# An encoder block on one core: two by two blocks with seven products in the in-projection, x turned on the host, and attention beside other matmuls

## The chip, the core and the metric

The kernel runs on 1 core of one Trainium2 chip. Its time is the device time of one launch in microseconds (us); work on the host does not count. Before the change it took 2023.58 us, the median of 3 runs (2023.04 to 2024.13). Five engines work side by side, each in the order of its own program: TensorE (PE, matmuls and transposes), VectorE (DVE), ScalarE (ACT), GpSimd (POOL) and SyncE (SP, which here only starts DMA transfers). They wait for each other through semaphores.

## The reference, cut to what matters

One layer of a bidirectional encoder on 512 tokens of width 2048, all in float32. Two mixers read one projection of the normalised input: A has 8 query heads on 2 key heads with rotary angles on normalised q and k; B has 8 heads whose three dilated windows are merged by their softmax denominators. Heads have 128 columns.

```
h = rmsnorm(x, g_mix[layer])
proj = jnp.einsum('bsd,de->bse', h, w_in[layer])            # 512 x 2048 by 2048 x 4608
qa, ka, va, qb, kb, vb = jnp.split(proj, offs, axis=-1)     # 1024, 256, 256, 1024, 1024, 1024 columns
...
out_a = rmsnorm(mixer_a(qa, ka, va, g_q_a[layer], g_k_a[layer]), g_out_a[layer])
out_b = rmsnorm(mixer_b(qb, kb, vb), g_out_b[layer])
mixed = jnp.concatenate([out_a, out_b], axis=-1)
x = x + jnp.einsum('bse,ed->bsd', mixed, w_out[layer])      # 2048 x 2048
h2 = rmsnorm(x, g_ffn[layer])
gate, up = jnp.split(jnp.einsum('bsd,df->bsf', h2, w_gate_up[layer]), 2, axis=-1)   # 2048 x 11264
x = x + jnp.einsum('bsf,fd->bsd', jax.nn.silu(gate) * up, w_down[layer])            # 5632 x 2048
return rmsnorm(x, g_final)
```

## The kernel before

**Three products for one.** Every float32 operand is split in two: ACT copies it rounded to the type fp32r (the high part), and DVE subtracts that copy from the original (the low part). `mm3` (L194 to L198) then multiplies high by high, high by low and low by high into one PSUM bank. So each weight tile costs one ACT pass, one DVE pass and three matmuls for each 128 rows of tokens.

**Seven products for eight.** The gate/up and down stages go further. They take their matrices as 2 x 2 blocks and compute the four blocks of a product with seven block products instead of eight, named m1 to m7. The sums of blocks on the activation side are made once per pair of rows (`pair_sums`, L656), those on the weight side for every tile (`ColBlock.weights`, L778). A form's 12 matmuls (two rows, two halves of the tokens, `mm3`) make one unit, and three pairs of PSUM banks, z, y and x, collect the seven products in the order of `CHAIN`; ACT copies a bank out (`snap`) where another block needs it too, and DVE adds the rest.

**The in-projection** does not do this. `in_chunk` (L534) takes 512 columns of w_in at a time, nine chunks, each 16 units (one for each 128 rows of w_in) of 12 matmuls for the four tiles of tokens. During the first chunk `x_transposes` (L256) turns x with PE, 128 columns at a time, ACT and DVE scale it by g_mix and split it into `arena`, and ACT and POOL sum its squares; the norm's factor is applied when a chunk leaves PSUM (`post_kvA`, `post_qA`, `post_vB`, `post_qkB`). The order is: k and v of A, q of A (two chunks), v of B (first half), q and k of B for heads 0 to 3 (two chunks), v of B (second half), q and k of B for heads 4 to 7.

**Attention** runs in the gaps between units. `push_head` (L489) puts the tasks of a head on a list, `side`, and the main loop takes one task after each unit: m0 (turn q; last value product of the head before the last, `fin`), tk (turn k), and four steps `ms(i)`, each with the scores of 128 queries of this head (`score`), the turning of a quarter of the weights of the head before (`pt`) and that head's value product before (`pv`). In `score`, DVE takes the row maximum out of PSUM, ACT the exponential with the row sum, DVE its reciprocal and the scaling of the row:

```
nc.vector.tensor_tensor_reduce(p, ps, mask[:, lo:lo + S], -1.0, 3e38, op0=OP.add, op1=OP.min, accum_out=nmx)
nc.scalar.activation(p, p, AF.Exp, bias=nmx, scale=-1.0, accum_out=z)
nc.vector.reciprocal(rz, z)
nc.vector.tensor_scalar(p, p, rz, None, op0=OP.mult)
```

All heads of A come first, then those of B; finished heads go to DRAM (`o_dram`) and come back scaled and split for **the output projection** (`out_chunk`, L583): four chunks for A's half of the rows, then four for B's, 8 units each. The last heads of B run beside the chunks of A. Behind each chunk of B, `h_side` (L682) turns the new x in tasks from the same list and makes the forms for the gate/up stage.

**What sets the order.** The whole order is written out in the program. `units` lists all units; `prepare(n)` (L1184) issues, ahead of unit n, the weight loads up to 24 (later 20) planned us ahead, ACT's high splits up to 10 (8.2) ahead and DVE's low splits one behind those. Planned lengths are 2.6 and 2.72 us a unit. Loads go through SP's queue, in order, each waiting for its buffer.

Of the kernel before, what the change touches and what calls it, by code (L numbers as in the profile page):

```python
# [24 lines left out]
KD = D // P  # L25
NC = D // 512
# [9 lines left out]
BRANCHES = ((128, 1), (512, 4), (2048, 16))  # L36

LOAD_AHEAD = 24.0
SPLIT_AHEAD = 10.0
SIDE_AHEAD = 13.0  # L40
UNIT_US = 2.6
FORM_US = 1.31
EVAC_WAIT = 3
LAST_WAIT = 2
# [3 lines left out]
PLAIN_WAIT = 5  # L48
SPILL_B = 6
RAWS = {"raw": 6, "a": 4, "b": 4, "s": 4, "d": 12, "home": NFF // 2}  # L50
W_TILES = {"wi": 12, "wo": 12}
# [4 lines left out]
ORDER = ("m1", "m4", "m5", "m3", "m2", "m7", "m6")  # L56

# [6 lines left out]
def encoder_block(ctx, tc, x, g_mix, w_in, g_q_a, g_k_a, g_out_a, g_out_b, w_out, g_ffn,  # L64
                  w_gate_up, w_down, g_final, c_ident, c_mask, c_axial, c_partial, out):
# [5 lines left out]
    sm = ctx.enter_context(tc.tile_pool(name="small", bufs=1))  # L71
# [12 lines left out]
    ring = [0]  # L84

    def wslot(tag):
        if tag == "wa":
            ring[0] += 1
            return home(16 + ring[0] % 12)
        return sp.tile([P, 512], F32R, tag=tag, bufs=W_TILES[tag], name=nm("w"))  # L90

# [3 lines left out]
    def small(base, n=4):  # L95
        return sm.tile([P, 16], F32, tag="t", bufs=24, name=nm(base))[:, :n]

    xs = [None] * KD

    def load_x(k):  # L100
        xs[k] = slot(f"x{k}", F32, (P, NT, P))
        nc.sync.dma_start(xs[k], x[0, :, k * P:(k + 1) * P].rearrange("(t p) c -> p t c", p=P))

    ident = cp.tile([P, P], F32, name="ident")
    gm = cp.tile([P, KD], F32, name="gm")
    gf = cp.tile([P, KD], F32, name="gf")
    go = cp.tile([P, KD], F32, name="go")
    mask = cp.tile([P, S + S - P], F32, name="mask")
    ropeb = cp.tile([P, 2, NT, PARTIAL], F32, name="ropeb")
    ones = cp.tile([P, 1], F32, name="ones")  # L110
    mhalf = cp.tile([P, 16], F32, name="mhalf")
    gqk = cp.tile([P, 2, HD], F32, name="gqk")
    arena = [sp.tile([P, n, KD // 2, 2, 256], F32R, tag=f"arena{n}", bufs=1, name=f"arena{n}") for n in (4, 3)]
    def form_home(m, i):
        return arena[m // 4][:, m % 4, i]

    def home(n):
        return form_home(n % 7, n // 7).rearrange("p a b -> p (a b)")

    load_x(0)  # L120
    nc.scalar.dma_start(ident, c_ident)
    nc.vector.memset(ones, 1.0)
    nc.vector.memset(mhalf, -0.5)
    warm = slot("warm", BF16, (P, 512))
    nc.vector.memset(warm, 0.0)
    nc.scalar.activation(slot("table")[:, :1], ones, AF.Copy)
    warm_ps = bank("warm")

    def warm_up(n):
        for _ in range(n):  # L130
            nc.tensor.matmul(warm_ps, warm[:, :P], warm, start=True, stop=True)

    def load_gain(dst, rows, eng):
        raw = slot("gain")[:KD, :P]
        lo = 0
        for src, n in rows:
            eng.dma_start(raw[lo:lo + n], src[0].rearrange("(k p) -> k p", p=P))
            lo += n

        def finish():  # L140
            ps = bank("gain")
            nc.tensor.transpose(ps[:, :KD], raw, ident[:KD, :KD])
            nc.scalar.activation(dst, ps[:, :KD], AF.Copy)
        return finish

    gm_ready = load_gain(gm, [(g_mix, KD)], nc.scalar)

    def row_bcast(vec, n):
        return bass.AP(tensor=vec.tensor, offset=vec.offset, ap=[[0, P], [1, n]])

    def load_consts():
# [1092 lines left out]
```

## Time and profile before

| what | value |
|---|---|
| median of 3 runs | 2023.58 us (2023.04 to 2024.13) |
| profiled execution | 2024.27 us, of which 2022.5 us from its first to its last instruction |
| in-projection on PE, first to last start | 7.1 to 514.5 us |
| output projection | 516.8 to 723.5 us |
| gate/up blocks | 723.8 to 1589.6 us |
| down projection | 1589.9 to 2013.3 us |

A group's row has its line, engine and operation, what is written from what, the shapes and the count, then busy time, the mean of one in ns, and the idle time of the engine ahead of them with what ended it. A row of the timeline has start and length in us, engine, line, and in brackets the idle time ahead of it. Matmuls overlap, so the distance between starts is their price, and not the length of one. These rows of the page show the other engines over the span, in 40 slices of about 51 us, as tenths:

```profile
DVE  5555755554654587877777777778778799788776
ACT  5324344444533554444444544545445545455464
PEclk9999999999999999999999999999999999999999
DMA  7322322223433536567567476575575997579855
```

DVE is busy for half of the time in the first fourteen slices, where attention runs, and for seven to nine tenths behind them; the clock that TensorE is granted is full throughout.

### The profile page before, as it was taken

How to read it: one execution, taken by the hardware profiler on the slowest of the kernel's cores; microseconds unless marked ns; L12 is line 12 of the kernel's file. 1: busy time of each engine (PE TensorE's matmuls, PEld its weight loads, DVE VectorE, ACT ScalarE, POOL GpSimd, SP SyncE). 2: the span in 40 equal slices, each digit the busy share in tenths (PEclk: the TensorE clock that was granted, in tenths of full speed). 3: DMA queues.
4: the chain of work that ended last, by engine and by line, in shares of the span. 5: the costliest groups of instructions: out<-in, count | busy, mean ns of one | idle time of the engine just before them, and what ended most of it. 6: DMA issues, size and time to landing. Idle time of an engine off the chain costs nothing.

```text
span 2022.5 us, 24151 instructions
## 1 busy us (share of the span) xinstructions
PE 2005.3 (99%) x9135; PEld 1653.4 (82%) x9135; DVE 1429.0 (71%) x1876; ACT 952.6 (47%) x1345; POOL 81.7 (4%) x86
## 2 busy tenths in 40 slices
PE   9999999999999999999999999999999999999998
PEld 7888888888888878888888888888888887888886
DVE  5555755554654587877777777778778799788776
ACT  5324344444533554444444544545445545455464
POOL 3100100000000000000000000000000001002000
PEclk9999999999999999999999999999999999999999
DMA  7322322223433536567567476575575997579855
GB/s 235 105 83 69 99 70 77 74 83 112 133 119 125 186 138 218 167 221 244 171 230 234 159 244 217 162 267 190 185 267 185 320 390 222 178 220 340 289 179 178
DMA packets 213140, 373.59 MB, mean 185 GB/s; under 512 B 12784, under 2 KB 57632, under 8 KB 212896
## 3 DMA queue, kind: packets, MB, share of 16 engines
q1 hardware_dynamic: 207104, 358.87, 53.4%
q0 software_dynamic: 3728, 9.44, 1.9%
q10 hardware_dynamic: 2192, 3.74, 0.5%
q8 instruction: 71, 1.16, 0.2%
q14 instruction: 45, 0.37, 0.1%
HBM read 335.57 MB, written 36.44 MB: 184 GB/s over the span
## 4 chain that ended last, share of the span: by engine, by line
PE 95%; DVE 3%; issue 1%; ACT 1%; DMA 0%; ACTq 0%; POOLq 0%; POOL 0%; DVEq 0%
PE zc L198 8%; PE zc L196 8%; PE zc L197 8%; PE pj L196 7%; PE pj L198 7%; PE pj L197 7%; PE yc L196 4%; PE yc L198 4%; PE yc L197 4%; PE zd L197 4%; PE zd L198 4%; PE zd L196 4%; PE pw L196 3%; PE pw L198 3%; PE pw L197 3%; PE yd L198 3%
## 5 line engine op out<-in xcount | busy, mean ns | idle before, releaser
L196 PE MATMUL zc<-twin,arena 128*128 128x512 f32 x704 | 277.8, 395 | 3.5 <-ACT arena L700 3.5
L198 PE MATMUL zc<-twin,arena 128*128 128x512 f32 x704 | 275.3, 391 | 0.0
L197 PE MATMUL zc<-twin,arena 128*128 128x512 f32 x704 | 274.6, 390 | 0.0
L750 ACT ACTIVATE twin<-stockb 128x1024 fp32r<-128x1024 f32 x168 | 178.3, 1062 | 191.1 <-PE zc L198 76.9
L754 DVE TENSOR_TENSOR twin<-stockb,twin 128x1024 fp32r<-128x1024 f32 x168 | 205.1, 1221 | 40.8 <-ACT twin L750 38.8
L196 PE MATMUL pj<-w,arena 128*128 128x512 f32 x576 | 229.2, 398 | 0.8 <-ACT w L234 0.8
L754 DVE TENSOR_TENSOR twin<-stocks,twin 128x1024 fp32r<-128x1024 f32 x126 | 154.2, 1224 | 103.6 <-ACT twin L750 103.2
L197 PE MATMUL pj<-w,arena 128*128 128x512 f32 x576 | 224.9, 390 | 0.9 <-DVE w L239 0.9
L198 PE MATMUL pj<-w,arena 128*128 128x512 f32 x576 | 225.3, 391 | 0.0
L750 ACT ACTIVATE twin<-stocka 128x1024 fp32r<-128x1024 f32 x124 | 131.5, 1061 | 170.9 <-PE xc L198 58.3
L754 DVE TENSOR_TENSOR twin<-stocka,twin 128x1024 fp32r<-128x1024 f32 x124 | 151.5, 1223 | 66.5 <-ACT twin L750 58.5
L750 ACT ACTIVATE twin<-stocks 128x1024 fp32r<-128x1024 f32 x126 | 133.4, 1059 | 133.1 <-PE yc L198 71.4
L196 PEld LDWEIGHTS zc<-twin,arena 128*128 128x128 f32 x704 | 132.4, 188 | 30.7 <-ACT arena L700 3.8
L198 PEld LDWEIGHTS zc<-twin,arena 128*128 128x128 f32 x704 | 132.4, 188 | 28.9 <-DVE arena L702 0.8
L197 PEld LDWEIGHTS zc<-twin,arena 128*128 128x128 f32 x704 | 132.6, 188 | 26.3
L239 DVE TENSOR_TENSOR w<-raw,w 128x512 fp32r<-128x512 f32 x176 | 130.9, 754 | 18.4 <-ACT w L234 11.9
L196 PE MATMUL yc<-twin,arena 128*128 128x512 f32 x352 | 138.6, 394 | 0.0
L198 PE MATMUL yc<-twin,arena 128*128 128x512 f32 x352 | 137.6, 391 | 0.0
L197 PE MATMUL yc<-twin,arena 128*128 128x512 f32 x352 | 137.5, 391 | 0.0
L197 PE MATMUL zd<-twin,form 128*128 128x512 f32 x348 | 135.5, 389 | 0.1
L196 PE MATMUL zd<-twin,form 128*128 128x512 f32 x348 | 135.6, 390 | 0.0
L198 PE MATMUL zd<-twin,form 128*128 128x512 f32 x348 | 135.4, 389 | 0.0
(222 smaller groups left out, 3879.6 us busy)
## 6 DMA issues: line engine op xcount, KB each, us to landing
stocks<-in_w_gate_up_dram SPq DMA_DIRECT2D x220, 512.0 KB, 4.9
stocka<-in_w_gate_up_dram SPq DMA_DIRECT2D x44, 512.0 KB, 7.4
stockb<-in_w_gate_up_dram SPq DMA_DIRECT2D x44, 512.0 KB, 7.2
stocka<-in_w_down_dram SPq DMA_DIRECT2D x44, 512.0 KB, 9.0
stockb<-in_w_down_dram SPq DMA_DIRECT2D x44, 512.0 KB, 7.7
stocks<-in_w_down_dram SPq DMA_DIRECT2D x44, 512.0 KB, 8.3
forms<-pair SPq DMA_DIRECT2D x22, 896.0 KB, 6.1
raw<-in_w_in_dram SPq DMA_DIRECT2D x38, 512.0 KB, 3.7
```

The costliest lines, as they stand in the source:

```text
L196: nc.tensor.matmul(dst, ah, bh, start=start, stop=False, skip_group_check=chained)
L197: nc.tensor.matmul(dst, ah, bl, start=False, stop=False, skip_group_check=chained)
L198: nc.tensor.matmul(dst, al, bh, start=False, stop=stop, skip_group_check=chained)
L239: nc.vector.tensor_tensor(self.w[1], self.src, f32(self.w[0]), op=OP.subtract)
L750: nc.scalar.activation(self.pair[:, :, 0], self.src, AF.Copy)
L754: nc.vector.tensor_tensor(self.pair[:, :, 1], self.src, f32(self.pair[:, :, 0]), op=OP.subtract)
```

## The change

**x.** The host hands over x turned (`c_xp`) and the three gains in columns (`c_gain`). `x_base` scales and splits the four blocks of a pair of rows, `x_sums` makes the four sums of blocks that the seven products need, and both go to SBUF as xbase and xsum. The squares of x come from its rows, read once more (`square_rows`).

**The in-projection.** Three of the nine chunks stay plain: k and v of A first, and the two of q of A, the last of all. Their units are now 24 matmuls long (`Std`, two rows of 128). The other six become three blocks of 1024 columns with seven products (`x_block`): v of B; q and k of B for heads 0 to 3; q and k of B for heads 4 to 7. Results of these blocks and of the first chunk are scaled, written to DRAM on POOL's queue and read back where attention needs them.

**Attention** starts behind the last block: heads of B first, then those of A. It runs beside the two chunks of q of A and the output projection, whose B chunks now come ahead of its A chunks. The main loop takes tasks at a rate: 1.5 for every 12 matmuls beside q, 1.6 beside B's chunks. A second list, `side2`, gives one more piece of work each time: tables, norm and rope of A. The scaling by the reciprocal (`weigh`) has left the score step; it comes one step later, every other one on ACT.

```diff
+X_AT = {"m1": (0, 1), "m4": (0, 2), "m2": (0, 3), "m5": (1, 0), "m6": (1, 1), "m7": (1, 2), "m3": (1, 3)}
+RATE_B, RATE_A = 1.5, 1.6
...
+    def x_sums(i, step):
+        ga, nga, gb = gm[:, 2 * i:2 * i + 1], ngm[:, 2 * i:2 * i + 1], gm[:, 2 * i + 1:2 * i + 2]
+        raw = xraw[i]
+        if step == 0:
+            w = xpart[i] = work_at(3072 + 1536 * (i % 2), 1536).rearrange("p (f c) -> p f c", f=6)
+            nc.scalar.activation(w[:, :2], raw[:, 2:], AF.Copy, scale=gb)
+        w = xpart[i]
+        if step == 1:
+            nc.vector.scalar_tensor_tensor(w[:, 2], raw[:, 0], ga, w[:, 0], op0=OP.mult, op1=OP.add)
+            nc.vector.scalar_tensor_tensor(w[:, 3], raw[:, 1], nga, w[:, 2], op0=OP.mult, op1=OP.add)
+            nc.vector.tensor_tensor(w[:, 4:], w[:, :2], w[:, 3][:, None, :].to_broadcast([P, 2, 256]), op=OP.subtract)
+        if step == 2:
+            nc.scalar.activation(xsum[:, :, i, 0], w[:, 2:], AF.Copy)
+        if step == 3:
+            nc.vector.tensor_tensor(xsum[:, :, i, 1], w[:, 2:], f32(xsum[:, :, i, 0]), op=OP.subtract)
...
+    def x_block(lo0, lo1, dst0, dst1):
+        box = ColBlock(w_in, 0, (lo0, lo1), KD // 4, x_form, 0)
...
+        box.after("m1", 0, snap("m1", 0, "c11"))
+        box.after("m7", 0, snap("m7", 1, "c22"))
+        box.after("m6", 0, snap("m6", 1, "c21"))
+        box.after("m2", 1, add("m2", 0, "c11"))
+        box.after("m2", 2, store(dst0, 0, "c11"))
...
+    x_block(VB, VB + 512, v_dram[0], v_dram[1])
+    x_block(QB, KB, q_dram[0], k_dram[0])
+    last_x = x_block(QB + 512, KB + 512, q_dram[1], k_dram[1])
...
+        def weigh(self, t):
+            p, rz = self.p[t], self.rz[:, t:t + 1]
+            nc.vector.reciprocal(rz, self.z[:, t:t + 1])
+            if t % 2 == 0:
+                nc.scalar.activation(p, p, AF.Copy, scale=rz)
+            else:
+                nc.vector.tensor_scalar(p, p, rz, None, op0=OP.mult)
...
+        def task(n, i):
+            cur = heads[n] if n < len(heads) else None
+            prev = heads[n - 1] if 0 < n <= len(heads) else None
+            prev2 = heads[n - 2] if n > 1 else None
+            if i == 0:
+                if cur:
+                    cur.tq()
+                if prev:
+                    prev.weigh(3)
+                if prev2:
+                    prev2.pv(3)
+                    prev2.fin()
+            elif i == 1:
+                if cur:
+                    cur.tk()
+            else:
+                t = i - 2
+                if cur:
+                    cur.score(t)
+                if prev:
+                    prev.pt(t)
+                    if t:
+                        prev.pv(t - 1)
+                if cur and t:
+                    cur.weigh(t - 1)
...
-    for kind in "AB":
+    for kind in "BA":
         for c in range(NC):
             out_chunk(kind, c)
...
+            first = [("m1", 0), ("m1", 1), ("m1", 2), ("m2", 0), ("m2", 1), ("m7", 0), ("m7", 1), ("m1", 3), ("m7", 2),
...
+    def pump(rate):
+        for k, (q, r) in enumerate(((side, rate), (side2, 1.0))):
+            credit[k] = min(credit[k] + r, 2.5)
+            while credit[k] >= 1 and q:
+                q.popleft()()
+                credit[k] -= 1
```

How tasks stand between units is decided by the loop. On PE, one gap in the last in-projection chunk of before (sc is a score bank, pt turned weights, o the value product, pj the in-projection's bank; one row for each instruction):

```order
L198 MATMUL pj_4150<-w_4016,arena_83 128x512
L196 MATMUL sc_4163<-kTh_4009,qTh_3975 128x512
L197 MATMUL sc_4163<-kTl_4010,qTh_3975 128x512
L198 MATMUL sc_4163<-kTh_4009,qTl_3976 128x512
L453 MATMUL pt_4172<-ident,p_3822 128x128
L453 MATMUL pt_4172<-ident,p_3856 128x128
L453 MATMUL pt_4172<-ident,p_3897 128x128
L453 MATMUL pt_4172<-ident,p_3934 128x128
L196 MATMUL o_4087<-pTh_4136,arena_83 128x512
L197 MATMUL o_4087<-pTl_4137,arena_83 128x512
L198 MATMUL o_4087<-pTh_4136,arena_83 128x512
L196 MATMUL pj_4147<-w_4053,arena_83 128x512
```

The value product there reads a pTl made in the gap before. One gap beside the first chunk of q of A in the changed kernel:

```order
L135 MATMUL pj_2644<-twin,xbase 128x512
L133 MATMUL sc_2657<-kTh_2631,qTh_2577 128x512
L135 MATMUL sc_2657<-kTh_2631,qTl_2578 128x512
...
L654 MATMUL pt_2664<-whole,p_2450 128x128
...
L133 MATMUL sc_2673<-kTh_2631,qTh_2577 128x512
...
L654 MATMUL pt_2680<-whole,p_2450 128x128
...
L133 MATMUL o_2689<-pTh_2669,vB_2155 128x512
L134 MATMUL o_2689<-pTl_2670,vB_2155 128x512
L135 MATMUL o_2689<-pTh_2669,vB_2156 128x512
L133 MATMUL pj_2641<-twin,xbase 128x512
```

Two score steps stand in one gap, and the value product reads the pTh and pTl that are made from pt_2664 of the same gap. Of the gaps with attention in the changed order, 11 are like this one, 9 have a score step and a head's first task with two products, 6 have two score steps with a product in each; the others hold one task or none.

On DVE, one gap of before (the row maximum in two instructions, reciprocal and scaling of the row, the low half of the turned weights, the low split of a unit):

```order
L443 ISA p_4126,nm_4032<-sc_4122,mask 128x512
L443 ISA nm_4032 128x1
L446 RECIPROCAL rz_4034<-z_4033 128x1
L447 TENSOR_SCALAR p_4126<-p_4126,rz_4034 128x512
L186 TENSOR_TENSOR pTl_4137<-pt_4131,pTh_4136 128x512
L239 TENSOR_TENSOR w_4095<-raw_3874,w_4094 128x512
```

And DVE's rows for the gap of the changed kernel that is shown above:

```order
L639 ISA p_2661,whole<-sc_2657,btab 128x512
L639 ISA whole 128x1
L125 TENSOR_TENSOR pTl_2670<-pt_2664,pTh_2669 128x512
L639 ISA p_2677,whole<-sc_2673,btab 128x512
L639 ISA whole 128x1
L125 TENSOR_TENSOR pTl_2686<-pt_2680,pTh_2685 128x512
L645 RECIPROCAL whole<-whole 128x1
L511 ISA ra_2695,whole<-kvr_2132 128x128
```

The low half of the turned weights now stands directly behind the maximum, the reciprocal and the scaling behind that, and a piece of `side2` (here the norm of k of A, L511) behind the gap's tasks.

996 lines of the change are left out of this document (516 added, 480 removed).

## The prediction

> **What bounds the kernel now.** I read the page first, then the windows, TensorE's groups and waits, and then the timeline at the four places where the change acts.
>
> ```profile
> span 2022.5 us, 24151 instructions
> PE 2005.3 (99%) x9135; PEld 1653.4 (82%) x9135; DVE 1429.0 (71%) x1876; ACT 952.6 (47%) x1345; POOL 81.7 (4%) x86
> PE 95%; DVE 3%; issue 1%; ACT 1%; DMA 0%; ACTq 0%; POOLq 0%; POOL 0%; DVEq 0%
> ...
> 400.00:475.00 75.00, 75.00 (x360) 61.90 (x359) 41.99 (x109) 32.59 (x68) 2.69 (x2) 1.00 0.25 78
> 850.00:900.00 50.00, 50.00 (x226) 41.36 (x225) 38.15 (x38) 22.23 (x25) 0.00 (x0) 1.00 0.74 249
> ```
>
> TensorE (PE) ends last: 95% of the chain, busy for 99% of the span. The windows (columns: window, its length, PE, PEld, DVE, ACT, POOL, granted clock, DMA share, GB/s) show why: with attention beside the in-projection, VectorE (DVE) is busy for 42 of 75 us, and in the gate/up blocks for 38 of 50. So PE work removed is time won, as long as DVE and ACT keep up. Whether they do is the question here, since the change puts attention beside a third of the in-projection matmuls that it had.
>
> **What PE loses.**
>
> ```profile
> L196 PE MATMUL pj<-w,arena 128*128 128x512 f32 x576 | 229.2, 398 | 0.8 <-ACT w L234 0.8
> L259 PE MATMUL xt<-ident,x 128*128 128x128 f32 x64 | 10.5, 291 | 0.0
> ...
> 711.45 0.39 PE L197 MATMUL pw<-w,arena 128*128 128x512 f32 x1
> 711.68 0.39 PE L198 MATMUL pw<-w,arena 128*128 128x512 f32 x1
> 711.91 0.60 PE L688 MATMUL x1t<-ident,x 128*128 128x128 f32 x4
> 712.26 0.48 PE L196 MATMUL pw<-w,arena 128*128 128x512 f32 x1
> 712.58 0.39 PE L197 MATMUL pw<-w,arena 128*128 128x512 f32 x1
> ```
>
> Matmuls overlap, so the price of one is the distance of starts, 0.23 us, not 0.39. Four transposes cost 0.35 to the next start, and that matmul's step is 0.32: 0.44 us together. The in-projection has 3 x 576 = 1728 matmuls. After, three chunks have 192 each and three blocks 7 x 4 x 12 = 336 each: 1584. That is 144 x 0.23 = **33.1 us** less. The 16 groups of xt go: 16 x 0.44 = **7.0 us**. The column sums and gain transposes are under 1 us; I leave them out.
>
> ```profile
> 742.89 0.60 PE L688 MATMUL x1t<-ident,x 128*128 128x128 f32 x4
> 747.02 0.80 PE L196 MATMUL zc<-twin,arena 128*128 128x512 f32 x1 [3.53 <-ACT arena L700]
> 747.61 0.63 PE L197 MATMUL zc<-twin,arena 128*128 128x512 f32 x1
> ...
> 752.71 0.48 PE L196 MATMUL yc<-twin,arena 128*128 128x512 f32 x1
> ...
> 7.12 0.78 PE L196 MATMUL pj<-w,arena 128*128 128x512 f32 x1
> ...
> 13.56 0.50 PE L197 MATMUL pj<-w,arena 128*128 128x512 f32 x1 [0.89 <-DVE w L239]
> 13.90 0.39 PE L198 MATMUL pj<-w,arena 128*128 128x512 f32 x1
> ```
>
> At the first gate/up block PE waits 3.53 us for the last h forms, and the next 12 steps take 5.69 us instead of 12 x 0.23 = 2.76: the matmuls run at about half pace. The new order has all transposes ahead of the second m2 unit and seven units of 2.76 us ahead of the first that needs those forms (six before). I take **6 us** won (bounds 0 and 6.4). The first matmul stands at 7.12 and waits on transposes of x; with x turned on the host it needs a load, one ACT and one DVE pass: about 1.2 us earlier, and the waits near 12 and 13.6 us have longer units over them: together **2.5 us** (bounds -5 and 3: rows of x are now read too, for the squares; 2 MB per 5.5 us unit stands against 332 GB/s, the most that a window at the start shows). Sum won: 33.1 + 7.0 + 6 + 2.5 = **48.6 us**.
>
> The three blocks themselves: per block DVE has 28 low splits, 16 subtractions and 6 evacuations on 77 us of PE, the same as a gate/up block, where the window above shows PE never idle at 38 of 50. I take nothing, with 0 to 5 us for three stream buffers where gate/up has four. The way of v, q, k through DRAM is hidden by the following blocks, except for the first pair, read one unit before it is turned: 2 us, bounds 0 and 8.
>
> **What packed attention costs.** One score step of before, in order of time:
>
> ```profile
> 402.84 0.39 PE L198 MATMUL sc<-kTh,qTl 128*128 128x512 f32 x1
> 403.07 0.60 PE L453 MATMUL pt<-ident,p 128*128 128x128 f32 x4
> 403.27 0.69 DVE L443 CUSTOM_DVE_ANT_0 p<-sc,mask 128x512 f32<-128x512 f32 x1 [0.27 <-PE sc L198]
> 404.06 0.72 ACT L445 ACTIVATE p<-p,nm 128x512 f32<-128x512 f32 x1 [1.98 <-DVE nm L443]
> 404.79 0.58 ACT L185 ACTIVATE pTh<-pt 128x512 fp32r<-128x512 f32 x1
> 404.91 0.16 DVE L446 RECIPROCAL rz<-z 128x1 f32<-128x1 f32 x1 [0.94 <-ACT p L445]
> 405.11 0.49 DVE L447 TENSOR_SCALAR p<-p,rz 128x512 f32<-128x512 f32 x1
> 405.51 0.68 DVE L186 TENSOR_TENSOR pTl<-pt,pTh 128x512 fp32r<-128x512 f32 x1
> 406.11 0.68 DVE L239 TENSOR_TENSOR w<-raw,w 128x512 fp32r<-128x512 f32 x1
> ```
>
> The maximum on DVE releases the exponential on ACT; behind that, in ACT's order, stands the high half of the turned p (pTh), which DVE's low half (pTl) needs, which the value product needs. Before, one such step stands between units of 12 matmuls, so nothing on PE waits. After, PE's order has two tasks in one gap, over and over, and the value product of the first stands in the same gap. From the end of sc's step (403.07) pTh starts at 404.79 and takes 0.58; pTl can then run 405.45 to 406.13, and PE goes on 0.1 later: 3.16 us. PE's own work until then is, for two score tasks, pt 0.44, sc 0.69, pt 0.44 and the first product's step 0.23: 1.80. It waits **1.36 us**. The same sum holds for a score task followed by a head's first task (pt, two products, qt). Where a product of an earlier step stands between as well, 2.49 is covered and 0.67 waited for. PE's order has 11, 9 and 6 such gaps: 20 x 1.36 + 6 x 0.67 = **31.2 us**.
>
> DVE has no such slack either. Its other work there:
>
> ```profile
> L754 DVE TENSOR_TENSOR twin<-stocka,twin 128x1024 fp32r<-128x1024 f32 x124 | 151.5, 1223 | 66.5 <-ACT twin L750 58.5 <-DMA stocks<-in_w_gate_up_dram 6.0 <-DMA stockb<-in_w_gate_up_dram 1.5
> L623 DVE SCALAR_TENSOR_TENSOR x<-pw,ro,x 128x512 f32<-128x512 f32 x32 | 22.0, 745 | 17.6 <-PE pw L198 17.6
> L446 DVE RECIPROCAL rz<-z 128x1 f32<-128x1 f32 x64 | 10.5, 164 | 56.8 <-ACT p L445 29.3 <-ACT p L440 27.5
> L311 DVE CUSTOM_DVE_ANT_0 ra<-qA 128x128 f32<-128x128 f32 x32 | 7.4, 287 | 6.3 <-ACT qA L362 6.3
> L319 DVE TENSOR_TENSOR ra<-qA,gsq 128x256 f32<-128x256 f32 x16 | 6.0, 418 | 0.0
> L327 DVE TENSOR_TENSOR qA<-qA,rq 128x512 f32<-128x512 f32 x8 | 5.5, 693 | 0.8
> ```
>
> In its new order DVE stands idle inside each step (maximum at 0, pTl only at 2.2): the wait that the reciprocal had (56.8 us over 64 steps, 0.9 each) becomes one of about 1.5 ahead of pTl, and nothing can fill it. A head of mixer B takes on DVE 4 x (2.2 + 0.6 + 0.2) + 2 x 0.4 + 3 x 0.65 for the q, k and o lows + 2 x 1.2 for two units' splits = 17.2 us. PE needs 4 x 2.76 for the units of four gaps, 4 x 1.82 for sc, pt and product and 2 x 0.44 for qt and kt = 19.2, and 21.9 with two waits. On top comes one side task a gap, 1.1 us (norm and rope of A: 4 x 0.29 + 2 x 0.42 + 3 x 0.69 = 4.1 us by durations, some 3.4 by starts, in three tasks). Walked through in DVE's order from the start of a head's first sc at 0: maximum at 0.9, pTl from 3.1; next maximum 3.7, pTl from 5.9, side task to 7.8. PE passes the first product at 4.3, twelve matmuls at 7.1, and its third sc is ready at 7.9: maximum 7.9, pTl from 10.1, weighing to 11.3, side task to 12.4, split to 13.6. The fourth sc was ready at 12.5, so this is 1.1 late; pTl is there at 16.6, PE ends the last product at 17.0, twelve matmuls at 19.8, kt at 20.2, twelve more at 22.9. So a head takes 22.9 us. Every second of heads 1 to 5 also has the rope of k (2 x 0.29 + 2 x 0.42, 1.2 by starts) ahead of its second maximum, and a split of v behind the third (1.2 and 0.5 of waiting for ACT): 25.1, and 0.8 carried into the next head. Over the 21.9, four heads by 1.0 and three by 4.0 are **16 us**. Beside the output projection the side tasks (13.6 us) and the evacuations (16 x 0.75 = 12 us) come on heads with 16 us on DVE and 18.1 on PE (3.75 gaps). By the same walk the tasks delay each of three heads by some 1.7 and the evacuations each of four chunks by 1.5: **11 us**. Two evacuations of q in front of ACT's exponentials, the first pair and the last head: **8 us**. These 35 us count each delay in full, though some fall where PE waits anyway; nothing and 35 are the ends, and I take **22**. Last, at the end of each of the four A chunks the turning of x1 now follows the last matmul at once and waits for its evacuation, 0.2 + 0.75: **3.6 us**.
>
> **Sum.** 31.2 + 22 + 3.6 = 56.8 lost against 48.6 won: +8.2. The profiled execution took 2024.27 us (span 2022.5 and 1.8 around it), so 2032.5 by its own time, and **2032 us** by the median of 2023.58, 0.7 below it. With the ends of the unknowns the forecast's own range is 2012 to 2052.
>
> **Rivals.**
> - *Backlogs hide.* Only the waits written into PE's order count: 48.6 - 31.2 - 3.6 gives 14 us won, 2010. For it: DVE's side work may slip into gaps while PE runs its 2.76 us. Against: DVE is in order, and 17.2 of 19.2 us is used before any of it. It decides from about 14 us of extra delay.
> - *PE hardly waits.* If the gaps' waits were absorbed too, 48.6 us is won: 1975. Against it stands the row of the reciprocal: DVE already waits for ACT in every step, with one step per gap.
> - *The clock falls.* After the 3.53 us wait PE ran 12 steps at half pace, 2.9 us lost. If each of the 20 waits did that: 58 us more, 2090. Against: after the 0.89 us wait at 13.56 the next start comes 0.34 us later and then at normal pace, and the new waits of 1.4 to 3 us lie between. The Trainium skill, page "TensorE: Matmul & The Clock Gate", section "A second HAM failure mode: psum-queue depth-cycling", says that frequent short idles between groups of matmuls can make the clock swing, while its Part 1 asks for an idle window of about 3.4 us; by the first rule this rival happens, by the second not. The trace bears out the second at 3.53 and 0.89 us, and shows nothing between.
> - That the matmuls are not saved is excluded: the order of the changed kernel has 1584 in the in-projection.
>
> **Chances.** Forecast 0.60 (slower 0.45, same 0.10, faster 0.05), hidden backlogs 0.25 (faster 0.21, same 0.04), PE hardly waiting 0.09 (faster), clock 0.06 (slower). A measurement tells 0.2%, 4 us, from no change. So faster 0.35, same 0.14, slower 0.51. The range leaves out the last two cases: 1990 to 2062.
>
> **What would show it.** Right: in the page of the changed kernel PE idle below 9 tenths between roughly 280 and 600 us and full before; waits of o at its second product on pTl, 1.4 us and longer, as the largest group; pTl behind pTh as DVE's largest wait; no wait of 3.5 us at the first gate/up block; clock 1.0 in the packed stage. Wrong: waits there of 35 us or less in all (backlogs hidden), steps of 0.43 us behind the waits (clock), or PE waiting for DMA in the first 50 us or in the three blocks.

## The result and the profile after

The changed kernel takes **2084.9 us** (median of 4 runs, 2084.0 to 2086.0) against 2023.9 for the kernel before: 1.030 times as long, with a 95% interval of 1.028 to 1.032. The forecast said slower, by 8 us; it is 61 us, and the time lies above the range.

The page of the changed kernel: its span, the engines' busy time, two of the rows in 40 slices (each slice is 52 us), the engines' shares of the chain that ended last, and one group of DVE.

```profile
span 2083.0 us, 23648 instructions
PE 1996.8 (96%) x8916; PEld 1630.4 (78%) x8916; DVE 1519.5 (73%) x1837; ACT 1010.4 (49%) x1292; POOL 79.0 (4%) x99
PE   7899998888799999999999999999999999999998
PEclk9999999999999999999999999999999999999999
PE 81%; DVE 10%; ACT 5%; issue 2%; DMA 1%; POOL 0%; SPq 0%; ACTq 0%; POOLq 0%; DVEq 0%
L125 DVE TENSOR_TENSOR pTl<-pt,pTh 128x512 fp32r<-128x512 f32 x64 | 44.2, 691 | 83.0 <-ACT pTh L124 83.0
```

PE has 219 instructions fewer, the removed matmuls and transposes among them, and is busy 8.5 us less. But the span is 60.5 us longer, and PE's share of the chain fell from 95% to 81%. The slices show two dents: the first two, and the seventh to the eleventh (310 to 570 us). Windows cut at the first matmul of each stage show them in full (columns: window, its length, PE, PEld, DVE, ACT, POOL, granted clock, DMA share, GB/s):

```profile
5.00:75.00 70.00, 53.06 (x194) 40.73 (x195) 45.39 (x61) 43.06 (x62) 2.99 (x3) 0.88 0.70 242
75.00:305.00 230.00, 229.02 (x1012) 189.20 (x1010) 168.03 (x157) 105.44 (x110) 7.70 (x15) 1.00 0.66 218
305.00:503.00 198.00, 165.45 (x748) 130.27 (x749) 128.06 (x325) 92.44 (x168) 21.08 (x25) 0.95 0.34 110
503.00:684.00 181.00, 163.91 (x767) 129.40 (x766) 107.56 (x215) 83.53 (x157) 16.67 (x14) 0.97 0.28 90
684.00:790.00 106.00, 100.34 (x455) 81.34 (x454) 52.65 (x71) 45.98 (x70) 3.19 (x2) 0.97 0.52 178
790.00:1650.00 860.00, 858.99 (x3864) 709.53 (x3863) 668.37 (x678) 417.15 (x476) 1.92 (x1) 1.00 0.65 214
```

They are the first chunk (k and v of A), the three blocks, q of A with heads, the output projection's B chunks with heads, its A chunks, and the gate/up blocks. The first chunk and the three stages from 305 to 790 us lose, the last of them least; the blocks and gate/up do not. A ledger, with PE's own time from steps of 0.2275 us a matmul (an estimate for undisturbed steps; the middle one of the gate/up blocks is 0.227, and the prediction rounds to 0.23), 1.82 a score task and 0.44 four transposes. The last column but one has the same stretch of work of the kernel before, against its own time, which there holds the turns of x:

| stage | lasts | PE's own time | over it | over it before | predicted loss |
|---|---|---|---|---|---|
| first chunk, 5.4 to 74.7 | 69.3 | 192 x 0.2275 = 43.7 | 25.6 | 4.3 (7.1 to 62.2) | -2.5, with the earlier start |
| three blocks | 230.8 | 1008 x 0.2275 = 229.3 | 1.5 | | 0 |
| heads, output projection, 305.6 to 789.6 | 484.0 | 1152 x 0.2275 + heads 127 + turns and sums 9 = 398 | 86 | 1.4 (62.2 to 723.8, with the other chunks) | 56.8 |
| gate/up, against 866.1 before | 860.6 | | 5.5 won | | 6 won |

The first matmul starts 1.7 us earlier, so the first chunk loses 21.3 - 1.7 = 19.6 us where 2.5 were to be won: 22 us of the miss. The blocks and the stages with heads lose 86 in place of 56.8: 29 us. With the matmuls and turns removed (32.8 and 7.0 us) and gate/up, this adds up to the 60.5 us of the span.

PE's longest waits in the whole run (what it was about to do, what it waited for: us in all, times, longest), with SP's at the first chunk:

```profile
PE o L133 <- ACT pTh L124: 31.1, 20, 3.6
PE pj L134 <- DVE twin L226: 14.6, 6, 6.5
PE cs L691 <- POOL acc L684: 7.8, 2, 4.2
PE o L134 <- DVE pTl L125: 6.1, 26, 0.4
PE qt L613 <- DVE qA L527: 5.7, 1, 5.7
PE x1t L870 <- DVE xrows L801: 2.1, 8, 0.4
...
SPq L322 <- DVE early_work L342: 29.1, 5, 9.0
```

**In the heads** PE waits at the value product's first matmul (L133), for ACT's high part of the turned probabilities. One such wait in the timeline (start, length, engine, line; in brackets the idle time ahead and what ended it):

```profile
386.30 0.69 DVE L639 CUSTOM_DVE_ANT_0 p<-sc,btab 128x512 f32<-128x512 f32 x1
387.03 0.72 ACT L641 ACTIVATE p<-p,whole 128x512 f32<-128x512 f32 x1 [3.65 <-DVE whole L639]
387.75 0.58 ACT L124 ACTIVATE pTh<-pt 128x512 fp32r<-128x512 f32 x1
388.38 0.50 PE L133 MATMUL o<-pTh,vB 128*128 128x512 f32 x1 [3.59 <-ACT pTh L124]
...
390.37 0.63 PE L135 MATMUL pj<-twin,xbase 128*128 128x512 f32 x1
390.80 0.63 PE L133 MATMUL pj<-twin,xbase 128*128 128x512 f32 x1
```

PE had turned the tile by 383.7; ACT stood idle 3.65 us, because the exponential ahead of the high part in its order waited for DVE's maximum, and DVE was busy until then with v's split, the rope of k and a weight split. Behind the wait the matmuls run at 0.43 us a step.

**In the first chunk** the timeline shows a loop:

```profile
14.51 0.49 DVE L342 SCALAR_TENSOR_TENSOR early_work<-early_work,whole 128x256 f32<-128x256 f32 x1
15.06 0.33 SPq L322 DMA_DIRECT2D early_work<-in_c_xp_dram  x1
15.44 0.43 SPq L201 DMA_DIRECT2D whole<-in_w_in_dram  x1
20.00 1.06 ACT L218 ACTIVATE twin<-whole 128x1024 fp32r<-128x1024 f32 x1 [1.95 <-DMA whole<-in_w_in_dram]
20.59 0.50 PE L134 MATMUL pj<-twin,xbase 128*128 128x512 f32 x1 [2.60 <-DVE twin L226]
20.96 0.71 ACT L338 ACTIVATE early_work<-early_work,whole 128x512 f32<-128x512 f32 x1
22.22 0.49 DVE L342 SCALAR_TENSOR_TENSOR early_work<-early_work,whole 128x256 f32<-128x256 f32 x1
```

DVE's sum (L342) frees one of three places for x pairs; SP loads the next pair (L322) and behind it a tile of weights (L201); ACT rounds those weights (L218) when they land, 4.5 us later; only behind that, in ACT's order, stands the first step of the next pair's sums (L338), which leads to the next L342. From 14.51 to 22.22 is 7.7 us, and PE needs 5.5 for a unit. By the distances of starts, PE's seven waits cost 18 of the 25.6 us; 31 matmul steps of 0.35 to 0.47 us behind them cost 6 more, at the granted clock of 0.88 of this window.

### The profile page after: what moved, and what is told of

Read it like the earlier page. It is cut to its first block, busy times and chain, and to the rows that moved or that the text cites. A ratio compares the mean times of both kernels' runs of the same rounds, so it can differ in the third digit from the quotient of the medians.

```text
span 2083.0 us, 23648 instructions
## 1 busy us (share of the span) xinstructions
PE 1996.8 (96%) x8916; PEld 1630.4 (78%) x8916; DVE 1519.5 (73%) x1837; ACT 1010.4 (49%) x1292; POOL 79.0 (4%) x99
## 4 chain that ended last, share of the span: by engine, by line
PE 81%; DVE 10%; ACT 5%; issue 2%; DMA 1%; POOL 0%; SPq 0%; ACTq 0%; POOLq 0%; DVEq 0%
PE zc L134 10%; PE zc L135 10%; PE zc L133 10%; PE yc L133 5%; PE yc L135 5%; PE yc L134 5%; PE zd L134 4%; PE zd L135 4%; PE zd L133 4%; PE yd L135 2%; PE yd L134 2%; PE yd L133 2%; PE xc L133 2%; PE xc L135 2%; PE xc L134 2%; PE pw L133 2%
## 5 line engine op out<-in xcount | busy, mean ns | idle before, releaser
L226 DVE TENSOR_TENSOR twin<-whole,twin 128x1024 fp32r<-128x1024 f32 x172 | 210.0, 1223 | 94.9 <-ACT twin L218 94.5
L133 PE MATMUL zc<-twin,arena 128*128 128x512 f32 x704 | 277.3, 394 | 0.0
L218 ACT ACTIVATE twin<-st1b 128x1024 fp32r<-128x1024 f32 x168 | 178.4, 1062 | 193.4 <-PE zc L135 72.6
L218 ACT ACTIVATE twin<-whole 128x1024 fp32r<-128x1024 f32 x172 | 181.9, 1058 | 162.5 <-PE yc L135 73.7
L226 DVE TENSOR_TENSOR twin<-st1b,twin 128x1024 fp32r<-128x1024 f32 x168 | 204.8, 1219 | 36.4 <-ACT twin L218 35.9
L218 ACT ACTIVATE twin<-st1a 128x1024 fp32r<-128x1024 f32 x124 | 131.6, 1061 | 170.1 <-PE xc L135 59.9
L226 DVE TENSOR_TENSOR twin<-st1a,twin 128x1024 fp32r<-128x1024 f32 x124 | 151.4, 1222 | 65.6 <-ACT twin L218 63.7
L133 PEld LDWEIGHTS zc<-twin,arena 128*128 128x128 f32 x704 | 132.2, 188 | 27.3 <-DVE s L940 0.4
L133 PE MATMUL yc<-twin,arena 128*128 128x512 f32 x352 | 138.0, 392 | 0.0
L133 PE MATMUL zd<-twin,form 128*128 128x512 f32 x348 | 135.6, 390 | 0.0
L134 PE MATMUL yd<-twin,form 128*128 128x512 f32 (+1 forms) x272 | 105.3, 387 | 0.9 <-DVE twin L226 0.9
L135 PE MATMUL yd<-twin,form 128*128 128x512 f32 (+1 forms) x272 | 105.1, 386 | 0.1
L133 PE MATMUL yd<-twin,form 128*128 128x512 f32 (+1 forms) x272 | 105.0, 386 | 0.0
L125 DVE TENSOR_TENSOR pTl<-pt,pTh 128x512 fp32r<-128x512 f32 x64 | 44.2, 691 | 83.0 <-ACT pTh L124 83.0
```

What stands on the lines that cost most here:

```text
L125: nc.vector.tensor_tensor(lo, src, f32(hi), op=OP.subtract)
L133: nc.tensor.matmul(dst, ah, bh, start=start, stop=False, skip_group_check=chained)
L134: nc.tensor.matmul(dst, ah, bl, start=False, stop=False, skip_group_check=chained)
L135: nc.tensor.matmul(dst, al, bh, start=False, stop=stop, skip_group_check=chained)
L218: nc.scalar.activation(self.pair[:, :, 0], self.src, AF.Copy)
L226: nc.vector.tensor_tensor(self.pair[:, :, 1], self.src, f32(self.pair[:, :, 0]), op=OP.subtract)
```

## The experiments

Three questions: what made the first chunk long, what made the heads wait, and whether both together are the whole miss. Times are medians against a kernel before of 2023.2 to 2023.8 us in the same series; "chunk" is the length of the first chunk, 69.3 us in the changed kernel. The edits are against the changed kernel.

### The first chunk

**e1_ring**: seven places for the x pairs.

```
+    xlate = once("xlate", [P, 4, 1024])
-        xraw[i] = work_at(1024 * (i % 3), 1024)...
+        at = xlate[:, i - 3] if 3 <= i < 7 else work_at(1024 * (i % 7), 1024)
```

> The x pairs get seven places in place of three (four of them a tile of their own), nothing else moves. Theory A (a loop through the ring of three: SP's load of pair n+3 waits for DVE's sums of pair n, the weight load behind it on SP is late, ACT's high part of that unit waits for the load and stands ahead of the sums of the next pair): SP's wait on the sums (29.1 us) is gone, the first chunk falls from 69.3 us to 44 to 50, the whole kernel to 2060 to 2068 us. Theory B (the loads cannot come faster, some 2 MB for each of four units): SP no longer waits for DVE, but PE then waits for DMA in the same places, the first chunk keeps over 63 us, the kernel 2078 to 2086. Theory C (ACT's own work, about 5.4 us for each of four units): half the gain, first chunk 54 to 60, 2069 to 2077.

Measured: 2111.0 us (1.043, 1.042 to 1.045), chunk 93.5. All three theories fell: it is 26 us *slower*. SP no longer waits for the sums, but for the squares (its queue's wait, then the timeline of such a round):

```profile
SPq L367 <- ACT xn L368: 48.9, 6, 17.0
...
25.14 1.37 SPq L367 DMA_DIRECT2D xn<-in_x_dram  x2
26.56 0.42 SPq L324 DMA_DIRECT2D xlate<-in_c_xp_dram  x1
27.08 0.38 SPq L201 DMA_DIRECT2D whole<-in_w_in_dram  x1
36.11 1.06 ACT L218 ACTIVATE twin<-whole 128x1024 fp32r<-128x1024 f32 x1 [9.95 <-DMA whole<-in_w_in_dram]
```

The row tiles (xn), whose squares ACT sums, are loaded ahead of the next pair and weights on SP. In the changed kernel the second two of them are issued at 15.92, ahead of the first square (25.7), so four places are at work, though the program asks for two; the memory planner had given them more. Here the second two wait for the first squares: two places. The load then waits for a square, the weights behind it, ACT's high part for the weights, and the next square behind that: 17 us a round.

**e1b_fewrows**: six of the eight row loads left out.

```
-        nc.sync.dma_start(xn, x[0, t * P:(t + 1) * P, ...])
+        if n < 2: nc.sync.dma_start(xn, x[0, t * P:(t + 1) * P, ...]); xns.append(xn)
+        xn = xns[n % 2]
```

> Six of the eight loads of rows of x for the squares (3 MB) are left out; the squares are taken again of the first two, so that r1 is not the reference's. Theory A (ring loop): the loop's period stays 7.5 to 7.7 us, only its one round of 10.5 us shortens: 2078 to 2084 us. Theory B (bandwidth): the first chunk comes down to 44 to 50 us, the kernel to 2060 to 2068.

Measured: 2083.2 us (1.029, 1.028 to 1.031), chunk 65.8. Bandwidth is out as the cause: with 3 MB less of loads the chunk is 3.6 us shorter, where theory B has some 20; the period stays 7.7 us, and only the one round of 10.6 us has shortened.

**e3_hi_late**: the weights' high part one unit later on ACT.

```
-        u.load_ahead = 11.0
+        u.load_ahead, u.ahead = 11.0, 6.0
```

> In the first chunk each unit's high part of the weights is issued on ACT one unit later (behind the sums of the x pair two units before, not ahead of them); loads, rings and SP's order stay. Theory A' (the loop: the high part waits for a load just issued and holds up the sums, which free the ring's place, for which SP's next loads wait; its period is a load's time plus ACT's and DVE's steps): the first chunk falls from 69 us to 46 to 55, the kernel to 2064 to 2074 us. Rival (the rings themselves, three x pairs and three weight tiles, are too short whatever ACT's order): the chunk keeps over 64 us, 2079 to 2087.

Measured: 2079.3 us (1.028, 1.026 to 1.029), chunk 60.6: between the two expectations. ACT's high part no longer waits for any load but the first, yet the period of the sums stays 7.7 us, since ACT's other wait is untouched (waits of the first 75 us):

```profile
ACT xsum L345 <- DVE early_work L343: 17.2, 8, 3.0
```

In its order ACT does 5.9 us of work for a unit with squares and stands 1.8 us at L345 for DVE's three steps of the sums: 7.7 again. A second loop of the same length lay behind the first. (The chunk gains 8.7 us and the kernel 5.6: the stages with heads took 488.6 us in place of 484.0, and 486 to 487 in most other runs of this section, though nothing in them was changed. Why is not shown.)

**e3b_ring_a**: the seven places again, four of them in the tiles of the first block's weights. The sums of pair 6 are then taken from a tile that those weights have already overwritten, so they are not the reference's.

```
+        at = early_a[:, i - 3].rearrange(...) if 3 <= i < 7 else work_at(1024 * (i % 7), 1024)
```

> The x pairs get seven places in place of three, four of them in tiles that exist already and lie idle in the first chunk (the first block's weights), so that no other ring loses memory, as the rings of the row tiles did in e1_ring. ACT's order stays. Theory A' (serial loop): the high part still waits for a load just issued, but the load no longer waits for the sums of the unit before: the chunk falls to 50 to 62 us, 2068 to 2080; as much is lost if the first block's loads, which now wait for x pairs, come late. Rival (the row tiles' loop of e1_ring is in the depth, not in the memory): the chunk is again some 93 us, 2105 to 2113.

Measured: 2110.9 us (1.043, 1.042 to 1.045), chunk 92.8, with the same waits as e1_ring (47.6 us of SP for the squares). The rival's number, but not for its reason: the third and fourth row loads are issued at 25.2 us, behind the first square (24.0), so the row tiles had two places once more, and the next two runs show what that costs. That the planner had given them the memory of the idle tiles is our reading; no run shows it.

**e10_ring5** and **e10b_rows2** give the row tiles memory of their own, four and two places, with five and three places for the x pairs.

```
+    xns = [once(f"xn{n}", [P, D // 2]) for n in range(4)]          # range(2) in e10b_rows2
...
-        xn = sp.tile([P, D // 2], F32, tag="xn", bufs=2, name=nm("xn"))
+        xn = xns[n % 4]                                            # n % 2
```

> The x pairs get five places in place of three, and the row tiles for the squares four places of their own (so many as the trace of the changed kernel shows; in e1_ring and e3b_ring_a they had two). Orders stay. If e1_ring was slow because the row tiles lost two places: no round of 17 us any more, the chunk 60 to 72 us (ACT's own loop of 7.7 us stays), 2070 to 2083 us. If a deeper x ring itself is what hurts: the chunk over 90 us, 2100 to 2113.

> The changed kernel with exactly two places for the row tiles, three for the x pairs. If the row tiles' places are what e1_ring lost: SP waits for the squares, ACT's high part for the load behind them, a round takes some 17 us, the chunk 90 to 100 us, 2103 to 2114 us. If it was the deeper x ring: 2082 to 2087, as the changed kernel.

Measured: e10_ring5 2083.3 us (1.030, 1.028 to 1.031), chunk 66.0; e10b_rows2 2111.4 us (1.044, 1.042 to 1.045), chunk 95.3. SP's wait in e10b_rows2:

```profile
SPq L367 <- ACT xn L368: 42.4, 6, 15.1
```

So the places of the row tiles, and not the depth of the x ring, cost those 26 us. A deeper x ring alone gains 3.3 us of the chunk: ACT's own loop stays, with 17.0 us of waits at the rounding of the sums in e10_ring5.

**e8b_sums_late** and **e8_both**: the rounding of the sums one unit later, alone, and with e3_hi_late.

```
+                late_sums(n - 1)          # x_sums steps 2 and 3, behind the squares of unit n
...
-            if n < KP:
-                x_sums(n, 2 * j)
-                x_sums(n, 2 * j + 1)
+            if n < KP and j == 0:
+                x_sums(n, 0)
+                x_sums(n, 1)
...
```

> In the first chunk the rounding of each x pair's sums (its step on ACT, which waits 1.8 us for DVE in every unit) is issued one unit later, behind the next pair's own high parts and the squares; the weights' high parts stay where they are. Two-loop theory (two loops of nearly the same 7.7 us: one of SP's load, ACT's high part that waits for it and the sums; one of ACT's own 5.9 us a unit and its 1.8 us wait for DVE; each alone hides the other): hardly a change, the chunk keeps 66 to 74 us, 2078 to 2087 us. If the wait for DVE was the whole loss: 2062 to 2072.

> e8b_sums_late and e3_hi_late together. Two-loop theory: with both loops open the period falls to ACT's own 5.9 us in the units with squares and to PE's 5.5 us in the others, the chunk to 46 to 56 us, the kernel to 2060 to 2071 us. If a third bound of the same size stands behind them (the loads, DVE's own work of some 5.6 us a unit): 2073 to 2080.

Measured: e8b_sums_late 2085.4 us (1.030, 1.028 to 1.032), chunk 66.0; e8_both 2071.5 us (1.023, 1.022 to 1.025), chunk 53.7. Alone they take 3.3 and 8.7 us off the chunk, together 15.7, where the sum would be 12: two loops that hide part of each other. (In e8b_sums_late the kernel gains nothing from its 3.3 us, by the heads' 3 us as above.) The window of e8_both's first chunk shows what is left:

```profile
5.00:59.00 54.00, 47.13 (x192) 37.34 (x193) 44.08 (x61) 42.09 (x61) 2.66 (x2) 0.94 0.88 310
```

DVE is busy for 44 of 54 us and ACT for 42, and at 310 GB/s the loads now run faster than the 242 that they reached in the slow order, with the DMA engines busy for 0.88 of the window (0.70 there). Which of these bounds what is left was not tested.

### The heads

**e2_exp**: ACT's exponential behind the high part of the head before.

```
                 if cur:
-                    cur.score(t)
+                    exp = cur.score(t)      # matmuls and maximum
                 if prev:
                     prev.pt(t)
+                if cur:
+                    exp()
```

> Within a task of the heads, ACT's exponential of the current head's row of scores is issued behind the high part of the previous head's turned probabilities, not ahead of it; PE, DVE and the gaps keep their order. Theory O (order on ACT: the high part waits behind an exponential that waits for DVE's maximum): the waits of the value product (31.1 on the high part, 6.1 on the low part) fall under 12 us in all, DVE's wait for the high part falls from 83 to under 30 us, the half-pace steps between 310 and 690 us go with them, and the kernel comes to 2040 to 2060 us. Theory L (DVE has more work in these stages than PE's time, whatever the order): the waits move to the low part or to the scores' banks, and the kernel keeps 2073 to 2086 us.

Measured: **2042.8 us** (1.010, 1.008 to 1.011), 42 us won by the place of one ACT instruction in a task. The waits of e2_exp:

```profile
PE cs L691 <- POOL acc L684: 8.3, 2, 4.7
PE o L134 <- DVE pTl L125: 5.4, 6, 1.7
PE qt L613 <- DVE qA L527: 4.4, 1, 4.4
PE o L133 <- DVE whole L639: 3.5, 4, 1.2
PE o L133 <- DVE pTl L125: 1.6, 4, 0.9
```

The value product's waits fell from 37.2 to 10.5 us, DVE's wait for the high part from 83.0 to 14.0, and the stages with heads from 484.0 to 444.4 us. PE has as many gaps with two tasks as in the changed kernel: by themselves they cost at most these 10.5 us.

**e4_nonorm** and **e6_exp_nonorm**: norm and rope of A left out, in the changed kernel and in e2_exp.

```
-        side2.extend((first, second))
+        return
```

> The norm and rope of A's q and k (some 43 us of DVE work, 35 of it on q beside the heads) are left out, so that heads of A are not the reference's; the order of all else stays. Theory O (order on ACT): the 5.7 us wait for the last turned q goes, and some of the backlog: 2066 to 2080 us; the value product still waits over 20 us. Theory L (DVE's work): the waits of the value product fall under 12 us, 2030 to 2055 us.

> e2_exp with the norm and rope of A's q and k left out, so that A's heads are not the reference's. Theory O (the order on ACT was the cause, DVE's work only fed it): the two gains (42 and 24 us) overlap, 2022 to 2036 us, from the 4.4 us wait for q, half of the 10.5 us of the value product and the half-pace steps behind them. Theory L (two separate losses): they add up, 2015 to 2021 us. DVE's work not at issue at all: 2039 to 2045.

Measured: e4_nonorm 2061.2 us (1.019, 1.017 to 1.020), a time between the two expectations, with 25.7 us of waits left at the value product, as theory O had it; e6_exp_nonorm 2029.2 us (1.003, 1.002 to 1.004). Without norm and rope DVE is busy 38 us less by its page (the 43 us of the expectation were an estimate). They cost 24 us in the old order and 14 in the new. The two gains are 42 and 24 alone, 56 together: they overlap, as theory O expected, but theory L has its share: with the order mended, DVE's side work still costs 14 us.

### Both

**e7_three**: e2_exp, e3_hi_late, and the last head's squares summed on PE.

```
+                if self.h < 7:
                     nc.gpsimd.tensor_tensor(acc[self.kind], acc[self.kind], sq, op=OP.add)
+                else:
+                    acc[self.kind, 7] = sq      # col_sums then multiplies both tiles by ones
```

> Three repairs together, all of the computation kept: e2_exp's order on ACT, e3_hi_late's order in the first chunk, and the last head's squares summed by PE (eight small products in place of four) in place of POOL's addition, for which PE waited 4.2 and 3.6 us. If the gains add up (42, some 17, some 5): 2015 to 2026 us, level with the kernel before (2023.8). If the first chunk's loss is not that loop: 2034 to 2040.

Measured: 2036.0 us (1.006, 1.005 to 1.008). PE's wait at the column sums fell only from 8.3 to 5.2 us, now for ACT's square: POOL's addition was not all of it. And e3_hi_late brought its 6 us, not 17.

**e9_all**: e2_exp, e8_both, `row_rms` as a later task of the heads' own list (in place of the kind of summing in e7_three), and A's norm and rope faster.

```
-            if self.h == 7:
-                side2.appendleft(lambda: row_rms(self.kind))
...
+        extra.setdefault((9, 3), []).append(lambda: row_rms("B"))
...
+        side.extend([lambda: None, lambda: None, lambda: row_rms("A")])
...
-        for k, (q, r) in enumerate(((side, rate), (side2, 1.0))):
+        for k, (q, r) in enumerate(((side, rate), (side2, 1.5))):
```

> All repairs, the whole computation kept: e2_exp's order on ACT, e8_both's order in the first chunk, the sums over the heads' squares asked for two or three steps later than their last addition (PE waited 8.3 us for it in e2_exp), and A's norm and rope issued at one and a half steps a gap in place of one (4.4 us of wait for q in e2_exp). If the gains add up (42, some 18, 8, 4 and the half-pace steps behind the waits): 2005 to 2020 us, faster than the kernel before (2023.8). If the first chunk keeps its loss: 2024 to 2036.

Measured: 2037.4 us (1.007, 1.006 to 1.008). Both waits at which it aimed are gone, but the chunk took 68.6 us: SP waits for the squares again (25.7 us), and the third and fourth row loads are issued only behind the first square (19.0 and 17.9 us), so the row tiles have two places in this kernel.

**e12_all**: e9_all with the row tiles in four tiles that are free then, and norm and rope at one step a gap.

```
-        xn = sp.tile([P, D // 2], F32, tag="xn", bufs=2, name=nm("xn"))
+        xn = early_a[:, n % 4].rearrange("p s c -> p (s c)")
```

> e9_all with four places for the row tiles made sure of (in the first block's weight tiles, which are loaded behind the last square), and A's norm and rope at one step a gap again. The first chunk 57 to 62 us as in e8_both (73.9 in e9_all), the stages with heads as in e7_three less its 5.2 us wait for the squares: 2016 to 2027 us, level with the kernel before. If the first chunk keeps over 70 us: 2032 to 2040.

(The 57 to 62 and 73.9 us in it are times of the chunk's end, not its length.) Measured: **2013.3 us**, 0.995 of the kernel before (0.994 to 0.997), 72 us under the changed kernel and 3 us under the range expected. Its page, and its windows of q of A and of the output projection's B chunks:

```profile
span 2011.6 us, 23647 instructions
PE 1972.4 (98%) x8916; PEld 1618.3 (80%) x8916; DVE 1520.7 (76%) x1837; ACT 1011.0 (50%) x1292; POOL 79.2 (4%) x99
```

```profile
290.00:460.00 170.00, 156.87 (x745) 124.44 (x744) 127.13 (x321) 92.91 (x168) 21.02 (x24) 0.99 0.38 127
460.00:620.00 160.00, 157.37 (x767) 127.44 (x766) 108.68 (x216) 84.75 (x158) 16.71 (x14) 1.00 0.31 103
```

PE has the same 8916 instructions as in the changed kernel. The chunk takes 53.5 us and the stages with heads 428.9, so 10 and 31 us over PE's own time, in place of 25.6 and 86: 71 us of the two together, which is the whole difference to the changed kernel. In e9_all the stages with heads took 439.4: running norm and rope denser costs some 10 us. There the scores wait 6.0 us for k's split, in place of 0.2.

**e13_weigh**: e12_all with all scalings of the probabilities on ACT.

```
-            if t % 2 == 0:
-                nc.scalar.activation(p, p, AF.Copy, scale=rz)
-            else:
-                nc.vector.tensor_scalar(p, p, rz, None, op0=OP.mult)
+            nc.scalar.activation(p, p, AF.Copy, scale=rz)
```

> e12_all with the other half of the scalings of the probabilities on ACT too (32 steps of 0.49 us on DVE become 32 of some 0.6 us on ACT). Theory L for what is left (DVE's work in the stages with heads): 4 to 10 us less than e12_all. Order alone: the same within 3 us, or slower where ACT's high parts now wait behind the scalings.

Measured: 2027.9 us (1.002, 1.001 to 1.003), 15 us *slower* than e12_all. DVE has less to do, yet the value product waits 17.7 us in place of 10.1, and the scores wait 3.7 us for k's split in place of 0.2. So work moved from DVE to ACT lengthens the chain through both engines more than it relieves DVE. Which step of it bounds what is left is not shown.

## Why the prediction missed

- **Removed matmuls and turns (33.1 and 7.0 us)**: right. In e12_all, where most waits are gone, the kernel is faster than before, and the ledger closes with these gains to within 0.5 us of its span.
- **First gate/up block (6 us)**: right; the 3.5 us wait is gone, the largest wait there is 0.7, and the blocks take 5.5 us less.
- **The start (2.5 us won)**: wrong, and the sign too: 19.6 us were lost, 22 us of the miss. The step spoke only of the first matmul, which does start 1.7 us earlier, of the waits near 12 and 13.6 us, and of the loads' rate (2 MB per unit against 332 GB/s, at most 5 us lost). e1b_fewrows shows that the rate did not matter. What counts is the program: x turned on the host puts three rings (x pairs, weight tiles, row tiles) and ACT's and DVE's sums into one circle, with a load's whole way in it. The order of the new code showed both loops of 7.7 us: each load's place, who frees it, and what stands ahead of that on its engine.
- **The blocks and the way through DRAM (0 and 2 us)**: right, 1.5 us over. (The 2 us were named and then left out of the sum; and 4 x 0.95 is 3.8, not 3.6. Neither matters here.)
- **Value product's waits in two-task gaps (31.2 us)**: the chain (maximum, exponential, high part, low part) was the right one, and 37.2 us were measured. But the place was off: PE waits at the first product, for the high part, 20 times up to 3.6 us, and only 0.23 at the second. The prediction let each exponential start on time and charged DVE's backlog apart, as its term of 22 us; in truth the backlog acts through this chain, since an exponential that waits for a late maximum holds back a high part that was ready. e2_exp cuts the link and takes 42 us back; the rest of DVE's work is worth 14 us (e6_exp_nonorm).
- **Other waits**: 7.8 us at the column sums were not seen at all, nor part of the 5.7 us for the last quarter of an A head's q. The turning of x1 cost 2.1 us instead of 3.6.
- **The clock**: given 6% as a rival, it came true in part. The forecast was a granted clock of 1.0; the windows say 0.95 to 0.97 in the stages with heads. Counting matmul steps of 0.35 to 0.47 us in the trace, there are 46 between 305 and 790 us, some 0.2 us each: 9 us of the 86. In the first chunk 31 more cost 6 us, at a clock of 0.88. The waits had been priced at their length alone. That the rival's 2090 us lies near the result is luck: it took 58 us of half pace, and some 15 were measured.
- **Hidden backlogs and PE hardly waiting** (34% together) fell for this order. The first one's 2010 us is near the 2013.3 of e12_all, which has the same work in another order, but with waits left and not for the reason that it gave.

The sum of the waits in the heads was close, 56.8 us predicted and 56.0 in the list of PE's waits from 305 to 790 us, and that is luck: the parts were 37.2 for 31.2, 2.1 for 3.6, and 16.7 us of others for the 22 of the backlogs. Nor is it what they cost. By the distances of starts 60 waits make 65 us; with 9 of half pace and some 12 of small steps, not taken apart, that is the 86. So two steps of the prediction failed. Its term for the start (2.5 us won) left the loops through the rings out, and its terms for the heads (31.2 and 22 us) kept DVE's backlog apart from the chain that it acts through and priced the waits without the slow steps behind them.

Still open: what the 31 us over PE's own time in e12_all consist of beyond some 18 us of listed waits.

## What to carry to other kernels

Where a change adds a stream of loads, walk each ring as a circle: who frees the place, what stands ahead of that instruction on its in-order engine, and whether that waits for a load of the same round. If it does, a unit costs a whole load, and two such circles of like length hide each other, so that mending one shows little. In a chain that crosses engines, issue the ready and urgent operation ahead of the one that still waits, and don't count on places that the memory planner gave beyond those asked for.

## What was not expected of the hardware

How long PE must stand idle before it runs at half pace varied. Two waits in the changed kernel, of 2.38 and 2.41 us:

```profile
373.78 0.50 PE L133 MATMUL o<-pTh,vB 128*128 128x512 f32 x1 [2.38 <-ACT pTh L124]
...
375.07 0.39 PE L133 MATMUL pj<-twin,xbase 128*128 128x512 f32 x1
375.30 0.39 PE L134 MATMUL pj<-twin,xbase 128*128 128x512 f32 x1
...
426.96 0.50 PE L133 MATMUL o<-pTh,vB 128*128 128x512 f32 x1 [2.41 <-ACT pTh L124]
...
429.42 0.78 PE L133 MATMUL pj<-twin,xbase 128*128 128x512 f32 x1
429.99 0.63 PE L134 MATMUL pj<-twin,xbase 128*128 128x512 f32 x1
```

Behind the first the steps are 0.23 us; behind the second they are 0.57, then 0.43 and 0.41, and 0.23 again from 430.83. So 2.4 us is enough at times. In e1_ring a wait of 1.73 us (at 426.34) was followed by seven steps of 0.43 too. The Trainium skill, page "TensorE: Matmul & The Clock Gate", section "Part 1: The HAM clock gate (the "warmup" mystery)", gives an idle window of about 3.4 us that runs freely. That the window runs freely could explain why equal waits differ; but a wait of 2.4 us does not fill it, so by its length the trace does not agree.
